# Half of the second key group contracted during the modulation's transfers

## The chip, the core and the metric

The program runs on one core of one Trainium2 chip. The metric is the device time of one execution in microseconds; lower is better. The core's engines are named as the profile names them: PE (matrix multiplications; PEld is its weight load), DVE (vector), ACT (scalar and activation), POOL (general purpose) and SP, whose only work here is to issue transfers. Each runs its own list of instructions in order, and they wait for each other through semaphores. All sums of products go through PSUM, which this kernel hands out in eight banks of 128x512 floats: four named `mm`, two named `sm` and two named `gd` in the stage that is changed.

## The reference

A two-layer backbone over 256 latent tokens and 256 context tokens of width 2048. What matters here is its very beginning: the modulation vectors of layer 0 are computed from `c` and `c_ctx` (a 2048 x 4096 part of `ada_w`), the normalised tokens are scaled and shifted by them, and the result is multiplied by the first columns of `ev_w_in`, the keys `ka` of the gated-delta heads.

```python
sh1, sc1, ... = split(silu(c) @ ada_w[0] + ada_b[0], 6)
h  = rmsnorm(x, norm_mix[0]) * (1 + sc1) + sh1        # 256 latent tokens
hc = the same with ctx and c_ctx                      # 256 context tokens
ka, va, kb, vb, a, b, qa, qb, za = split(h @ ev_w_in) # ka: 1024 columns
k  = l2norm(silu(depthwise_conv(ka)))                 # then the gated delta rule
y  = concat(delta_heads(k, v, q, gates), neighbourhood_attention(qb, kb, vb)) @ ev_w_out
```

Layer 0 goes on with a feed-forward network, layer 1 is a short convolution and another feed-forward network. Everything is float32; a product is made of three matmuls on a high and a low part of both factors (`hi*hi`, `hi*lo`, `lo*hi`).

## The kernel before

**The start.** The 4096 columns of `ada_w` that make shift and scale are taken in eight blocks of 256 + 256 columns. `start_block(b)` (L457) brings one block from memory in four pieces of 128x4x2x256, each by two transfers of 512 KB that SP issues (L463), into a ring of four buffers `araw0`, and multiplies each piece with `cT2` into one `gd` bank (L466). `start_tokens(b)` (L470) turns the bank into what the tokens need: DVE copies it to `mrow` (L472), four small matmuls put the numbers onto partitions (L477), three DVE instructions make shift and scale (L479 to L483), and for the two feature tiles k = 2b, 2b+1 PE transposes the four token tiles (L487), ACT applies shift and scale (L490), and DVE writes the high and low part of `h` (L491, L492). In the profile `araw0` is shown as `araw`, and the high and low parts of h are `hlhi`, `hllo` (latent) and `hchi`, `hclo` (context), `h` for k = 0.

**The contraction.** `fm_stream` (L288) multiplies h with 512 columns of weights for one feature tile k per step: four `mm` banks, and for each bank three weight blocks times two token halves, so 24 matmuls of 128x128 by 256 columns in a step (at k = 0 four of them cover both halves at once). Sixteen steps make one stream; the last two steps are emitted together (TAIL). Its weights come in transfers of 128x1024 floats, 512 KB, issued by SP (L225) into a ring of four `raw` buffers, and are split by ACT (L168, `whi`) and DVE (L234, `wlo`) into rings of three buffers.

In the loop over the blocks (L642) each turn runs `start_tokens(b)`, then two steps of the first stream `s0` (keys, columns 0 to 511) for the tiles just made, then `start_block(b+1)`. After the loop the last two steps of `s0` run (L656), and then the second stream (columns 512 to 1023, L662) runs alone. Each finished stream hands its four banks to `head_evac` (L550), which copies them to `hst`, and puts ten pieces of work (convolution, SiLU, transposes, norms) into a list; `drive` (L393) takes one piece from the list behind each step of whatever stream runs next.

**After it.** The gates of the delta rule (L693), `flush()` of the list (L742), the streams for `va`, `qa` and the others, the chunk matrices and inverses of the delta rule, its scans (L889: matmuls L907, L916, L927, L935, L949 in order), the neighbourhood attention head by head (L1062, L1087), the normalised output of the delta heads (L994, transposes from `o_t`), and the output projection, whose first quarter needs attention heads 0 to 3 and whose second quarter needs the delta heads.

**What sets the order.** The code is written in the order above, but the order on each engine is not that of the code: a scheduler that runs when the program is built simulates a timeline and lets an instruction go ahead of earlier ones when its inputs and buffers are ready there. The order is then fixed.

Of the kernel before, what the change touches and what calls it, by code (L numbers as in the profile page):

```python
# [23 lines left out]
F32 = mybir.dt.float32  # L24
# [80 lines left out]
def body(tc, x, c, ctx, c_ctx, ada_w, ada_b, norm_mix, norm_ffn, ffn_w_gate, ffn_w_up, ffn_w_down,  # L105
# [42 lines left out]
    def mmt():  # L148
        return mm.tile([128, 512], F32, name="mm", tag="mm")
# [135 lines left out]
                        evac(ti, n, ps[ti][n])  # L285
            yield

    def fm_stream(segs, ks, ws, evac):  # L288

        ps = [None] * 4  # L290
        for i, group in grouped(((k, (k, hi, lo)) for k, hi, lo in w_steps(segs, ks)), len(ks)):
            for f in range(4):
                if i == 0:
                    ps[f] = mmt()
                for g, (k, hi, lo) in enumerate(group):
                    a, b = hi[:, f * 128:(f + 1) * 128], lo[:, f * 128:(f + 1) * 128]
                    if i == 0:
                        PE.matmul(ps[f][:, 0:len(ws) * 256], a, h0[:, 0:len(ws) * 256], start=True, stop=False)
                    for j, (wt, mv) in enumerate(((a, h_hi), (a, h_lo), (b, h_hi))):
                        for n, w in enumerate(ws):  # L300
                            if j or i:
                                PE.matmul(ps[f][:, n * 256:(n + 1) * 256], wt, mv(w, k), start=False,  # L302
                                          stop=i == len(ks) - 1 and g == len(group) - 1 and j == 2 and w == ws[-1])
                if i == len(ks) - 1:
                    evac(f, ps[f])
            yield
# [83 lines left out]
            f, args = later.pop(0)  # L390
            f(*args)

    def drive(stream, pump=None, n=1):  # L393
        for _ in stream:
            if later:
                f, args = later.pop(0)
                f(*args)
            if pump:
                pump(n)
# [56 lines left out]

    def start_block(b):  # L457

        pr = gdt()
        for g in range(0, KT, 4):  # L460
            raw = sp.tile([128, 4, 2, 256], F32, name="araw0", tag="araw0", bufs=4)
            for s in range(2):
# [4 lines left out]
                          start=g == 0, stop=g == KT - 4)  # L467
        return pr

    def start_tokens(b, pr):  # L470
        mrow = sp.tile([128, 512], F32, name="mrow", tag="mrow", bufs=2)
        DVE.tensor_copy(mrow, pr)  # L472
        p = smt()
        for s in range(2):
            for f in range(2):
# [5 lines left out]
        DVE.scalar_tensor_tensor(sc0[:, kk, :], p[:, 4:8].rearrange("p (k w) -> p k w", w=2), 1.0,  # L481
                                 bT[:, 16 + 2 * b:18 + 2 * b, None].to_broadcast([128, 2, 2]), op0=OP.add, op1=OP.add)
        DVE.tensor_tensor(sc0[:, kk, :], sc0[:, kk, :], g_mix[0][:, kk, None].to_broadcast([128, 2, 2]), op=OP.mult)  # L483
        for k in range(2 * b, 2 * b + 2):
            p = smt()
            for t in range(4):
                transpose(p[:, t * 128:(t + 1) * 128], xn[:, t, k * 128:(k + 1) * 128])  # L487
            for w in range(2):
                m = sp.tile([128, 256], F32, name="modt", tag="modt", bufs=4)
                ACT.activation(m, p[:, w * 256:(w + 1) * 256], AF.Identity, bias=sh0[:, k, w:w + 1], scale=sc0[:, k, w:w + 1])  # L490
                DVE.tensor_copy(h_hi(w, k), m)  # L491
                DVE.tensor_tensor(h_lo(w, k), m, h_hi(w, k), op=OP.subtract)  # L492

    def token_stats():

# [54 lines left out]
    def head_evac(n, q, c0, done, sums):  # L550
# [1 line left out]
        st_ = {}  # L552

        def f(i_, p):
            st_[i_] = kvp.tile([128, 512], F32, name="hst", tag="hst", bufs=4)[:, 0:n * 128]
            copy(st_[i_], p[:, 0:n * 128])
            if i_ < 3:
                return
# [79 lines left out]

    sums = start_block(0)
    token_stats()  # L640
    s0 = fm_stream([(wv, C_KA, 512)], ks, [0, 1], ka_evac(0))
    for b in range(8):  # L642
        start_tokens(b, sums)
        if b < 7:
            next(s0), next(s0)
            sums = start_block(b + 1)
    st.close()
    rstk = Stack()
# [5 lines left out]
    ACT.dma_start(alog, ev_a_log.rearrange("o d h -> o (d h)").to_broadcast([128, 16]))  # L654
    ACT.dma_start(dtb, ev_dt_bias.rearrange("o d h -> o (d h)").to_broadcast([128, 16]))
    drive(s0)  # L656


    pump = Pump([ada_job(adap, 0, 2, "row", width=512, bufs=AB), ada_job(adap, 0, 3, "sh", width=512, bufs=AB),
                 ada_job(adap, 0, 4, "sc", gamma=g_ffn[0], width=512, bufs=AB)], 1, 1)  # L660

    drive(fm_stream([(wv, C_KA + 512, 512)], ks, [0, 1], ka_evac(1)))  # L662


    abstk = Stack()
# [719 lines left out]
```

## Time and profile before

| what | value |
|---|---|
| median of three runs | 2850.53 us (2845.95 to 2851.98) |
| the profiled execution: its time / its span | 2844.8 us / 2842.7 us |
| outside the span | 2.1 us |
| mean granted clock of PE | 0.988 |
| DVE busy, share of the span | 1902.5 us, 67% |
| ACT busy, share of the span | 1292.9 us, 45% |
| transfers, mean over the span | 239 GB/s |

A row of a group has the line, the engine, the operation, what is written and read, shapes and count; then the busy time in total and the mean of one instruction in ns. A row of a window has its bounds and length, then for PE, PEld, DVE, ACT and POOL the busy time and the number of instructions, then the clock granted to PE, the mean busy share of the transfer engines and GB/s. A row of the chain of waits has the start, the length and what the chain ran through.

### The profile page before, as it was taken

What the parts mean: (1) busy time and instruction counts of PE and PEld (TensorE: products, weight loads), DVE (VectorE), ACT (ScalarE), POOL (GpSimd) and SP (SyncE); (2) the same over time, 40 slices, a digit from 0 to 9 for tenths busy, and PEclk for the clock granted to TensorE, in tenths of its full rate; (3) what the DMA queues carried; (4) which work ended last, traced back from release to release, by engine and by line L of the source; (5) the groups of instructions that cost most, each with busy time, mean ns of one, the idle gap of its engine ahead of it and who ended that gap; (6) DMA issues with size and microseconds to landing.
All of it is one profiled execution on the core that took longest, in us unless ns stands there. A gap on an engine that the chain in (4) does not pass through costs nothing.

```text
span 2842.7 us, 40317 instructions
## 1 busy us (share of the span) xinstructions
PE 2726.7 (96%) x15113; PEld 2281.4 (80%) x15113; DVE 1902.5 (67%) x2599; ACT 1292.9 (45%) x1893; POOL 51.0 (2%) x77
## 2 busy tenths in 40 slices
PE   6899999989989999999999999999999999999997
PEld 3699989888767787888888878888878888888886
DVE  3387767857667887766677768786677544445565
ACT  3267543222354444444445554444444444444554
POOL 0000001000000000000000000000000000000000
PEclk9999999999999999999999999999999999999999
DMA  9955478777758799977788658997569666656663
GB/s 346 311 177 165 141 218 257 236 225 237 210 170 269 253 334 333 326 262 261 264 305 282 199 181 287 318 320 267 185 236 320 216 187 180 192 186 216 191 192 125
DMA packets 284926, 680.77 MB, mean 239 GB/s; under 512 B 57273, under 2 KB 97313, under 8 KB 283323
## 3 DMA queue, kind: packets, MB, share of 16 engines
q1 hardware_dynamic: 262148, 652.48, 69.6%
q10 hardware_dynamic: 22583, 25.73, 2.9%
q8 instruction: 118, 1.93, 0.3%
q14 instruction: 77, 0.63, 0.1%
HBM read 657.63 MB, written 20.48 MB: 239 GB/s over the span
## 4 chain that ended last, share of the span: by engine, by line
PE 66%; DMA 18%; DVE 10%; issue 3%; ACT 2%; SPq 1%; POOL 0%; ACTq 0%; DVEq 0%; POOLq 0%
PE mm L276 16%; PE mm L273 16%; PE mm L274 16%; DMA araw<-in_ada_w_dram 12%; PE mm L302 8%; DVE acc L321 3%; DVE wlo L234 3%; PE sm L187 2%; PE mm L282 2%; PE mm L284 2%; PE mm L283 2%; DMA br<-in_ev_rpb_dram 1%; DMA acc<-in_ada_b_dram 1%; DMA raw<-in_od_w_in_dram 1%; PE gd L466 1%
## 5 line engine op out<-in xcount | busy, mean ns | idle before, releaser
L234 DVE TENSOR_TENSOR wlo<-raw,whi 128x1024 fp32r<-128x1024 f32 x800 | 972.3, 1222 | 476.0 <-ACT whi L168 463.7
L168 ACT ACTIVATE whi<-raw 128x1024 fp32r<-128x1024 f32 x800 | 841.6, 1058 | 907.6 <-PE mm L276 669.4
L321 DVE SCALAR_TENSOR_TENSOR acc<-araw,cT,acc 128x1024 f32<-128x1024 f32 (+1 forms) x416 | 431.2, 1037 | 229.7 <-DMA araw<-in_ada_w_dram 196.3
L274 PE MATMUL mm<-wlo,fhi 128*128 128x512 f32 x1232 | 475.9, 392 | 0.7 <-DVE wlo L234 0.7
L273 PE MATMUL mm<-whi,fhi 128*128 128x512 f32 x1232 | 474.7, 395 | 0.0
L276 PE MATMUL mm<-whi,flo 128*128 128x512 f32 x1232 | 392.9, 393 | 0.0
L274 PEld LDWEIGHTS mm<-wlo,fhi 128*128 128x128 f32 x1232 | 231.5, 188 | 50.7 <-DVE wlo L234 1.4
L276 PEld LDWEIGHTS mm<-whi,flo 128*128 128x128 f32 x1232 | 231.0, 188 | 50.2
L273 PEld LDWEIGHTS mm<-whi,fhi 128*128 128x128 f32 x1232 | 231.6, 188 | 47.9
L273 PE MATMUL mm<-whi,ahi 128*128 128x512 f32 x672 | 259.8, 392 | 0.0
L274 PE MATMUL mm<-wlo,ahi 128*128 128x512 f32 x672 | 259.5, 391 | 0.0
L276 PE MATMUL mm<-whi,alo 128*128 128x512 f32 x672 | 209.7, 392 | 0.0
L302 PE MATMUL mm<-hllo,whi 128*128 128x256 f32 x640 | 181.2, 287 | 0.0
L302 PE MATMUL mm<-hlhi,wlo 128*128 128x256 f32 x600 | 169.7, 288 | 1.8 <-issue 1.4
L302 PE MATMUL mm<-hlhi,whi 128*128 128x256 f32 x600 | 167.2, 289 | 1.0 <-DVE hlhi L491 1.0
L171 ACT ACTIVATE ahi<-prodT 128x256 fp32r<-128x256 f32 x176 | 73.2, 417 | 194.7 <-PE mm L274 186.4
L274 PEld LDWEIGHTS mm<-wlo,ahi 128*128 128x128 f32 x672 | 126.2, 188 | 27.5
L273 PEld LDWEIGHTS mm<-whi,ahi 128*128 128x128 f32 x672 | 126.2, 188 | 27.2
L276 PEld LDWEIGHTS mm<-whi,alo 128*128 128x128 f32 x672 | 126.1, 188 | 27.3
L273 PE MATMUL mm<-whi,dhi 128*128 128x512 f32 x336 | 126.0, 395 | 2.4 <-DVE u_t L1309 1.6
L274 PE MATMUL mm<-wlo,dhi 128*128 128x512 f32 x336 | 127.8, 393 | 0.0
L302 PEld LDWEIGHTS mm<-hllo,whi 128*128 128x128 f32 x640 | 124.1, 194 | 0.5
(391 smaller groups left out, 4014.5 us busy)
## 6 DMA issues: line engine op xcount, KB each, us to landing
araw<-in_ada_w_dram SPq DMA_DIRECT2D x288, 512.0 KB
raw<-in_ffn_w_down_dram SPq DMA_DIRECT2D x176, 512.0 KB
raw<-in_ffn_w_gate_dram SPq DMA_DIRECT2D x160, 512.0 KB
raw<-in_ffn_w_up_dram SPq DMA_DIRECT2D x160, 512.0 KB
raw<-in_ev_w_in_dram SPq DMA_DIRECT2D x112, 512.0 KB
araw<-in_ada_w_dram SPq DMA_DIRECT2D x192, 256.0 KB
raw<-in_od_w_in_dram SPq DMA_DIRECT2D x96, 512.0 KB
raw<-in_ev_w_out_dram SPq DMA_DIRECT2D x32, 512.0 KB
```

The source lines that it names most:

```text
L168: ACT.activation(dst, src, AF.Copy)
L171: ACT.activation(hi, src, AF.Copy)
L187: return PE.transpose(dst, src, ident[:n, :n])
L234: DVE.tensor_tensor(lo, raw, hi, op=OP.subtract)
L273: PE.matmul(ps[ti][n], a, hi[:, n * 512:(n + 1) * 512], start=first, stop=False)
L274: PE.matmul(ps[ti][n], a, lo[:, n * 512:(n + 1) * 512], start=False, stop=False)
L276: PE.matmul(ps[ti][n], b, hi[:, n * 512:(n + 1) * 512], start=False, stop=last)
L282: PE.matmul(ps[ti][n], lh(t), hi[:, c_], start=False, stop=False)
L283: PE.matmul(ps[ti][n], lh(t), lo[:, c_], start=False, stop=False)
L284: PE.matmul(ps[ti][n], ll(t), hi[:, c_], start=False, stop=hi is group[-1][0])
L302: PE.matmul(ps[f][:, n * 256:(n + 1) * 256], wt, mv(w, k), start=False, stop=i == len(ks) - 1 and g == len(group) - 1 and j == 2 and w == ...
L321: DVE.scalar_tensor_tensor(acc, raw, cT[:, k:k + 1], acc, op0=OP.mult, op1=OP.add)
```

## The change

A second stream, `s1`, contracts columns 512 to 767 (half of the second key group) in the loop as well. It needs two banks, and takes them from `gd`; the sums of `start_block` move from `gd` to `sm`. `start_tokens` gets a generator, `both`, that alternates one step of `s0` and one of `s1`, and draws from it at four places: behind the copy to `mrow`, behind the scale, and behind each of the two feature tiles. In block b these are the steps for k = 2b-2 and 2b-1, a block later than before; in block 0 there is nothing to draw. After the loop the last two steps of `s0` and of `s1` run, and then the other half of the second group (columns 768 to 1023) as a stream of 256 columns, behind which `drive` takes a piece of the list only every second step. A step of a 256-column stream has 12 matmuls; its weight transfers have the same 128x1024 floats, now four feature tiles of 256 columns. The buffers `hst` become six.

```diff
-    def fm_stream(segs, ks, ws, evac):
+    def fm_stream(segs, ks, ws, evac, bank=None):
-        ps = [None] * 4
+        nf = sum(s[2] for s in segs) // 128
+        ps = [None] * nf
...
-            for f in range(4):
+            for f in range(nf):
                 if i == 0:
-                    ps[f] = mmt()
+                    ps[f] = (bank or mmt)()
...
-    def drive(stream, pump=None, n=1):
-        for _ in stream:
-            if later:
+    def drive(stream, pump=None, n=1, every=1):
+        for i, _ in enumerate(stream):
+            if later and i % every == every - 1:
...
     def start_block(b):
-        pr = gdt()
+        pr = smt()
...
-    def start_tokens(b, pr):
+    def start_tokens(b, pr, beside):
         mrow = sp.tile([128, 512], F32, name="mrow", tag="mrow", bufs=2)
         DVE.tensor_copy(mrow, pr)
+        next(beside, None)
         p = smt()
...
         DVE.tensor_tensor(sc0[:, kk, :], sc0[:, kk, :], g_mix[0][:, kk, None].to_broadcast([128, 2, 2]), op=OP.mult)
+        next(beside, None)
         for k in range(2 * b, 2 * b + 2):
...
                 DVE.tensor_tensor(h_lo(w, k), m, h_hi(w, k), op=OP.subtract)
+            next(beside, None)
...
-            st_[i_] = kvp.tile([128, 512], F32, name="hst", tag="hst", bufs=4)[:, 0:n * 128]
+            st_[i_] = kvp.tile([128, 512], F32, name="hst", tag="hst", bufs=6)[:, 0:n * 128]
...
-    s0 = fm_stream([(wv, C_KA, 512)], ks, [0, 1], ka_evac(0))
+    ka = [ka_evac(q) for q in range(2)]
+    s0 = fm_stream([(wv, C_KA, 512)], ks, [0, 1], ka[0])
+    s1 = fm_stream([(wv, C_KA + 512, 256)], ks, [0, 1], ka[1], gdt)
+
+    def in_turn(*streams):
+        while True:
+            for s_ in streams:
+                next(s_)
+                yield
+
+    both = in_turn(s0, s1)
     for b in range(8):
-        start_tokens(b, sums)
+        start_tokens(b, sums, both if b else iter(()))
         if b < 7:
-            next(s0), next(s0)
             sums = start_block(b + 1)
...
     drive(s0)
+    drive(s1)
...
-    drive(fm_stream([(wv, C_KA + 512, 512)], ks, [0, 1], ka_evac(1)))
+    drive(fm_stream([(wv, C_KA + 768, 256)], ks, [0, 1], lambda f, p: ka[1](f + 2, p)), every=2)
```

Line numbers behind L300 are one to fifteen higher in the changed kernel. Three places show what becomes of it on the engines.

**PE, between the sums of one block and those of the next** (block 2 of the loop). `cT` times `araw` are the sums of a block, `sm<-cs,mrow` the small matmuls of `start_tokens`, `sm<-cs,xn` the transposes of the tokens; `mm` and `gd` rows with `whi` or `wlo` are steps of `s0` and `s1`. Before:

```order
L466 MATMUL gd<-araw_421,cT_120 32x512 x4
L466 MATMUL gd<-araw_428,cT_120 32x512 x4
L466 MATMUL gd<-araw_435,cT_120 32x512 x4
L477 MATMUL sm<-cs,mrow 128x2 x4
L187 MATMUL sm<-cs,xn 128x128 x8
L466 MATMUL gd<-araw_533,cT_120 32x512 x4
L302 MATMUL mm<-hlhi,whi 128x256 x4
```

After, block 7, where the last sums are followed by the rest of the contraction:

```order
L303 MATMUL mm<-hlhi,wlo 128x256
L480 MATMUL sm<-cs,mrow 128x2 x4
L187 MATMUL sm<-cs,xn 128x128 x4
L303 MATMUL mm<-hchi,wlo 128x256
...
L303 MATMUL gd<-hlhi,wlo 128x256
L187 MATMUL sm<-cs,xn 128x128 x4
L303 MATMUL gd<-hchi,wlo 128x256
L303 MATMUL mm<-hlhi,whi 128x256 x4
```

Before, the small matmuls stood directly behind the last sums of their block, and all 48 matmuls of `s0` behind the transposes. Now stream matmuls stand between the last sums and the small matmuls (21 to 26 of them), between the two groups of transposes, and between the sums of the next block; 72 of them belong to a block.

**SP, around the last piece of the modulation's columns.** `araw` with 128x4x256 is a transfer of a block, `raw` a transfer of weights. Before:

```order
L463 DMA araw_1023<-in_ada_w_dram 128x4x256 x2
L463 DMA araw_1030<-in_ada_w_dram 128x4x256 x2
L225 DMA raw<-in_ev_w_in_dram 128x2x512 x2
L320 DMA araw<-in_ada_w_dram 128x512 x3
L317 DMA acc<-in_ada_b_dram 1x512
```

After:

```order
L225 DMA raw<-in_ev_w_in_dram 128x4x256
L464 DMA araw_1117<-in_ada_w_dram 128x4x256 x2
L464 DMA araw_1124<-in_ada_w_dram 128x4x256 x2
L464 DMA araw_1131<-in_ada_w_dram 128x4x256 x2
L464 DMA araw_1138<-in_ada_w_dram 128x4x256 x2
L225 DMA raw<-in_ev_w_in_dram 128x4x256 x2
L225 DMA raw<-in_ev_w_in_dram 128x2x512
L321 DMA araw<-in_ada_w_dram 128x512 x3
```

Counted from the top of SP's list, 12 transfers of weights stood ahead of the last piece of `araw` before, and 14 do now.

**PE, at the end of the delta rule's scans.** `gd<-state,kT`, `gd<-state,qT`, `gd<-R,xdT` and `gd<-vn,AT` are the four matmul groups of the last scan step, `kb,qb` are scores of the attention, `PT,vb` its values, and `mm` rows with `yhi` or `ylo` are the first quarter of the output projection. Before:

```order
L916 MATMUL gd<-state,qT 128x128 x4
L927 MATMUL gd<-R,xdT 128x128 x4
L1101 MATMUL sm<-PT,vb 128x256 x4
L1077 MATMUL sm<-kb,qb 128x512
L1078 MATMUL sm<-bq,cs 128x256
L949 MATMUL gd<-vn,AT 128x128 x4
...
L273 MATMUL mm<-whi,yhi 128x512 x4
L274 MATMUL mm<-wlo,yhi 128x512 x2
L276 MATMUL mm<-whi,ylo 128x512 x2
```

After:

```order
L276 MATMUL mm<-whi,ylo 128x512 x2
L187 MATMUL sm<-cs,s 128x128 x4
L964 MATMUL gd<-vn,AT 128x128 x4
L922 MATMUL gd<-state,kT 128x128 x4
L187 MATMUL sm<-cs,s 128x128 x4
L931 MATMUL gd<-state,qT 128x128 x4
L942 MATMUL gd<-R,xdT 128x128 x4
L1116 MATMUL sm<-PT,vb 128x256 x4
L964 MATMUL gd<-vn,AT 128x128 x4
L1092 MATMUL gd<-kb,qb 128x512
```

Before, the 48 matmuls of the output projection's first quarter (of 512 columns each) stood behind the last `vn,AT` of the scans. Now they stand ahead of the last `vn,AT` but one, and behind the scans only attention is left.

## The prediction

> **What bounds the kernel now.** I read the page's engine shares first, then windows, the chain of waits, and the waits of PE and SP inside the stage that is changed.
>
> ```profile
> PE 2726.7 (96%) x15113; PEld 2281.4 (80%) x15113; DVE 1902.5 (67%) x2599; ACT 1292.9 (45%) x1893; POOL 51.0 (2%) x77
> 60.00:120.00 60.00, 54.07 (x418) 37.24 (x417) 19.37 (x52) 12.17 (x20) 0.00 (x0) 0.97 1.08 351
> 40.00:140.00 100.00, 89.96 (x672) 62.16 (x673) 38.15 (x100) 23.07 (x39) 4.01 (x3) 0.98 1.01 328
> 140.00:193.00 53.00, 53.00 (x443) 52.80 (x442) 41.88 (x68) 33.66 (x80) 0.00 (x0) 1.00 0.63 193
> 480.00:720.00 240.00, 221.34 (x1851) 198.69 (x1850) 161.79 (x292) 63.82 (x121) 9.80 (x12) 0.97 0.77 236
> 720.00:960.00 240.00, 219.85 (x1046) 175.09 (x1046) 166.94 (x309) 116.69 (x225) 2.07 (x3) 0.96 0.67 211
> ```
>
> PE is busy 96% of the span, and the change neither adds nor removes a matmul. So the time can only fall by PE idle time that goes. While the modulation's columns arrive (40 to 140 us) PE is idle 10.0 of 100 us, with the transfer engines full at 351 GB/s. In the stage behind it (140 to 193, the second key group) it is never idle. Most other idle time before 960 us lies in the delta rule and the attention: 18.7 us in one window, 20.1 us in the next.
>
> ```profile
> 54.82 1.02 PE sm L477 x8
> 67.18 1.02 PE sm L477 x8
> 69.22 9.48 DMA araw<-in_ada_w_dram
> 97.13 1.04 PE sm L187 x8
> 132.61 2.76 PE gd L466 x24
> 135.39 0.70 DVE mrow L472
> 136.23 1.02 PE sm L477 x8
> 138.78 6.20 PE mm L302 x48
> 169.66 23.02 PE mm L302 x192
> ```
>
> These are rows of the chain. L477, the small matmuls, marks each block: from block 2 (67.18) to block 7 (136.23) five blocks take 69.05 us, **13.8 us each**. PE's own work in a block is 48 stream matmuls of 23.02/192 = 0.120 us (5.76 us), 32 records of sums at 2.76/24 = 0.115 us (3.68), the small matmuls (1.02) and the transposes (1.04): **11.5 us**. The chain runs through transfers of `araw` there. PE has 2.3 us to spare per block, and the transfers set the pace.
>
> **The change, part by part.**
>
> *Matmuls moved.* Of the 432 stream matmuls that stood behind block 7's small matmuls, 283 remain (counted from the orders; a 512-column matmul counts as two). That takes 149 x 0.120 = 17.9 us from the tail. The price is paid in the blocks: block 1 has 66 ahead of its small matmuls instead of 48 (+2.2 us, from 54.8 to 57.0), and from block 1 to block 7 stand 485 - 66 = 419. If PE never waits, block 7's small matmuls start at 57.0 + 419 x 0.120 + 6 x (3.68 + 1.02 + 1.04) = 57.0 + 50.2 + 34.4 = 141.6, that is 5.4 us later than 136.2. The tail then takes 283 x 0.120 + 1.0 + 1.0 + 2 (small matmuls, transposes, and those of the first heads) = 38.0 us. The second key group ended at 169.66 + 23.02 = 192.7 and would end at 179.6: **At most 13.1 us** earlier.
>
> *Transfers moved.* Two more weight loads stand ahead of the last `araw`.
>
> ```profile
> araw<-in_ada_w_dram SPq DMA_DIRECT2D x64, 512.0 KB
> 124.78 10.34 SPq L225 DMA_DIRECT2D raw<-in_ev_w_in_dram  x2
> SPq L463 <- PE gd L466: 22.0, 8, 3.8
> ```
>
> 2 x 0.524 MB at the 351 GB/s of the window is **3.0 us**. The last sums ended at 135.4; they would end at 138.4, and 26 stream matmuls (3.1 us) now stand between them and the small matmuls: 141.5. The limit by transfers and the limit by PE fall on the same point, so neither has slack. The new loads have the shape 128x4x256 that `araw` has (two of them to a piece), and those run at 351 GB/s, so I add nothing for shorter runs. SP already waits for PE's sums to free an `araw` buffer, 22.0 us in eight waits, at most 3.8; a transfer takes 9.5 us to land (the 69.22 row), so PE can free a buffer some microseconds late before the engines run dry. From nothing to 3.8 us for each of six blocks; I take nothing, as the transfer share is full in spite of those waits.
>
> *What fills the gaps.*
>
> ```profile
> PE sm L477 <- DVE mrow L472: 4.7, 5, 1.0
> PE gd L466 <- DMA araw<-in_ada_w_dram: 3.7, 4, 1.8
> PE sm L187 <- DVE xn L505: 1.0, 2, 0.5
> PE mm L302 <- DVE hlhi L491: 1.0, 2, 0.5
> L490 ACT ACTIVATE modt<-sm,sh,sc 128x256 f32<-128x256 f32 x32 | 15.7, 563 | 35.5 <-PE sm L187 35.5
> ```
>
> PE's waits between 40 and 140 us are for the copy `mrow` (4.7 us), for `araw` (3.7 us) and for h. The copy takes 0.70 us and has 21 to 26 matmuls in front of its reader now, so those 4.7 us go. h is used later, so those waits go too. The waits for `araw` remain where transfers are late. The sums' new place in `sm` adds a wait: the bank is free only when ACT has read it (two instructions of 0.56 us). Behind it on PE stand the sums, hence SP's next transfers. In the order, stream matmuls stand between; bounds 0 and 1.1 us per block, and I take 0, nearest to the stream matmuls that cover it.
>
> *The weight splits.*
>
> ```profile
> L234 DVE TENSOR_TENSOR wlo<-raw,whi 128x1024 fp32r<-128x1024 f32 x800 | 972.3, 1222 | 476.0 <-ACT whi L168 463.7
> L168 ACT ACTIVATE whi<-raw 128x1024 fp32r<-128x1024 f32 x800 | 841.6, 1058 | 907.6 <-PE mm L276 669.4
> ```
>
> ACT and DVE need 1.06 + 1.22 = 2.3 us for a split, and two streams share three buffers. The second stream reuses the buffer that it has just finished, so its split falls between two of its steps; there the order has 24 to 34 other stream matmuls (2.9 us or more). Four such places: 0 if covered, 9.1 us if each stands bare. They also leave DVE less to do later: 41.9 us of 53 in the tail, less about four splits (4.9) is 37.0 of the 38.0 us that the tail now lasts. DVE becomes nearly full there, with pieces of `head_evac` ahead of splits.
>
> For all of this I let 4 us of the 13.1 remain as waits (a number chosen between 0 and 9.1): **-9.0 us** at the end of the second key group, nine tenths of the 10.0 us of idle time that the window records.
>
> *What comes after.* The gates of the delta rule and all behind them stand later in PE's order. The first matmul of the gates has 911 stream matmuls before it now, and will have 1061; the first inverse 1976, then 2175. By 0.120 us that is 18.0 and 23.9 us later, less the 9.0 won: the delta rule starts 9 to 15 us later than before (its gates at 220 + 9 = 229).
>
> ```profile
> 220.04 1.26 PE sm L732 x12
> 744.39 1.05 PE L927 MATMUL gd<-R,xdT 128*128 128x128 f32 x8
> 803.93 1.06 PE L907 MATMUL gd<-state,kT 128*128 128x128 f32 x8
> 807.84 1.16 PE L927 MATMUL gd<-R,xdT 128*128 128x128 f32 x8 [0.59 <-DVE R L910]
> 813.84 1.13 PE L949 MATMUL gd<-vn,AT 128*128 128x128 f32 x8 [1.82 <-DVE o_t L921]
> 842.42 1.11 PE gd L187 x4
> ```
>
> The scans must end before the output projection can go on (842.4, transposes of the normalised output, 28.6 us behind the last scan matmul). Before, the first quarter of that projection (96 half-width matmuls, 11.5 us) filled this gap. In the new order it stands ahead of the last scan step, which fills the scans instead and leaves the gap emptier. Price: 0 if the scan steps simply run closer, 11.5 us if nothing replaces it. The last step took 813.84 - 803.93 = 9.9 us, while steps from 744.4 to 807.8 took 63.5/4 = 15.9 us: they were spread by other work, so they can run closer. I take the lower part: **+3.0 us**.
>
> *Sum.* -9.0 + 3.0 = -6.0 us: 2844.8 - 6.0 = 2838.8 for the profiled execution. That execution was 5.7 us under the median of 2850.5, and the change is compared with runs like the median: **2844.5 us**. The rest of the kernel behind 960 us has the same order but for single rows; nothing there.
>
> **A rule beside a row.**
>
> ```profile
> 110.00:120.00 10.00, 10.00 (x64) 6.79 (x57) 2.70 (x8) 1.61 (x4) 0.00 (x0) 0.86 1.09 353
> ```
>
> PE's granted clock was 0.86 here and 0.97 from 60 to 120. The Trainium skill, "TensorE: Matmul & The Clock Gate", section "What's actually happening", says that an idle window of about 3.4 us drops the clock to half. No wait of PE in this stage lasted over 1.8 us, so the trace has drops where the rule has none. If the denser order removes all of them, 0.03 x 60 = 1.8 us more is won; this enters the first rival alone.
>
> **The rivals.**
>
> *All of it stays.* The delta rule catches up at no cost and the waits are few: -13.1 - 1.8 = -14.9 at the extreme, typically -11: 2839.5. For it: 38.8 us of idle time between 480 and 960 that a moved chain could use. Against it: two limits at the same point.
>
> *Given back.* The start wins 9 us, and the scans, later in the order, return 7 to 9 of the 11.5: -1, 2849.5. For it: 28.6 us between scans and projection with one filler fewer. This includes that the change doesn't do what it says, because PE waits for `araw` where it waited before.
>
> *Slower.* One mechanism, the delta rule's chain. It starts up to 15 us later than before; if its steps can't run closer than their 15.9 us, the whole lateness reaches 842 us in place of the win: +6 to +15, I put +7: 2857.5. It decides once the lateness at the scans' start is more than the steps can make up, 4 x (15.9 - 9.9) = 24 us at best. Against it: that margin.
>
> **How the numbers follow.** Forecast -6 has 0.40, "all stays" 0.15, "given back" 0.30, "slower" 0.15. About 0.2%, 5.7 us, is what a measurement of this kernel can tell from no change. Forecast cases lie between -3 and -9; three quarters of them under -5.7 count as faster: 0.30 + 0.15 = 0.45. Same: 0.10 + 0.30 + 0.02 of the slower case = 0.42. Slower: 0.13. The range takes in -15.5 and leaves the worst of the last rival out, +5.5: 2835 to 2856.
>
> **What would show it.** Block marks (small matmuls) about 14.2 us apart and block 7's near 142; the last transposes and 192 stream matmuls of the second key group over by 184; PE idle between 40 and 140 at 3 us or less; the first gates' matmuls near 229; the transposes of the normalised output by 836. Wrong, if block marks are 15 us or more apart, if SP's waits for PE's sums exceed 22 us by much, if PE waits for `wlo` between 140 and 185, or if the normalised output comes at 842 or later.

## The result, and the profile after

| | before | after |
|---|---|---|
| median of six runs | 2846.98 us (2842.55 to 2851.98) | 2863.76 us (2856.03 to 2871.37) |
| ratio of the times, 95% interval | | 1.0053 (1.0038 to 1.0069) |
| profiled execution: time / span | 2844.8 / 2842.7 us | 2856.03 / 2854.2 us |
| mean granted clock of PE | 0.988 | 0.985 |

The changed kernel is **slower by 0.53%**; the forecast was 2844.5 us, with 2856 as the upper end. The profiled execution is the fastest of the six, and its span is 11.5 us longer than the one before. In the experiments below, one execution (of e10) took 9226.19 us; it is in no ratio.

First the page's engine line and windows of the changed kernel: bounds and length, busy time and instructions of PE, PEld, DVE, ACT and POOL, then PE's clock, the transfer engines' share and GB/s.

```profile
PE 2730.8 (96%) x15113; PEld 2282.0 (80%) x15113; DVE 1898.4 (67%) x2599; ACT 1298.7 (45%) x1897; POOL 52.7 (2%) x77
60.00:120.00 60.00, 58.51 (x460) 43.12 (x456) 19.20 (x50) 12.49 (x20) 0.00 (x0) 0.97 1.01 324
40.00:140.00 100.00, 97.25 (x749) 70.06 (x753) 37.52 (x92) 22.73 (x37) 0.00 (x0) 0.98 1.03 331
140.00:193.00 53.00, 53.00 (x447) 51.04 (x440) 40.74 (x64) 29.12 (x68) 4.02 (x3) 1.00 0.49 146
140.00:340.00 200.00, 193.41 (x1594) 189.20 (x1587) 156.58 (x332) 142.49 (x315) 13.98 (x21) 0.99 0.52 160
340.00:440.00 100.00, 87.14 (x1052) 84.32 (x1050) 65.50 (x106) 38.72 (x57) 2.97 (x4) 0.91 0.71 211
440.00:960.00 520.00, 478.04 (x3258) 410.50 (x3257) 358.92 (x666) 195.47 (x375) 21.07 (x31) 0.96 0.72 225
```

The same view of the kernel before, for the windows that the prediction doesn't show:

```profile
140.00:340.00 200.00, 195.97 (x1620) 194.03 (x1619) 156.53 (x328) 134.51 (x304) 8.81 (x18) 0.99 0.52 158
340.00:440.00 100.00, 95.50 (x1201) 92.30 (x1200) 73.67 (x124) 46.99 (x71) 4.96 (x8) 0.98 0.73 225
440.00:960.00 520.00, 479.20 (x3199) 411.39 (x3199) 361.26 (x666) 196.66 (x378) 19.54 (x28) 0.96 0.72 225
```

The start does what was hoped: PE idle between 40 and 140 us falls from 10.0 to 2.75 us. From 140 to 340 us idle time grows by 2.6, and **from 340 to 440 us from 4.5 to 12.9 us, with the clock at 0.91 in place of 0.98**. In that one window PE does about 87.14 x 0.91 = 79 us of full-speed work, where it did 95.50 x 0.98 = 94: some 14 us are lost there. From 440 to 960 us the idle time is equal within 1.2 us. Over the span idle time grows from 116.0 to 123.4 us, and the same matmuls are 4.1 us longer busy: together the 11.5 us.

Next PE's marks in time: the small matmuls (L480) of blocks 1, 2 and 7, the first matmul behind the second key group (L692), the first of the gates (L747), the last scan step (L964) and the transposes of the normalised output.

```profile
55.50 0.95 PE L480 MATMUL sm<-cs,mrow 128*128 128x2 f32 x8
71.92 0.95 PE L480 MATMUL sm<-cs,mrow 128*128 128x2 f32 x8
...
146.78 0.95 PE L480 MATMUL sm<-cs,mrow 128*128 128x2 f32 x8
184.81 0.28 PE L692 MATMUL sm<-h,abw 128*64 128x256 f32 x1
227.88 0.53 PE L747 MATMUL sm<-g_t,cs 128*128 128x32 f32 x4
839.04 1.05 PE L964 MATMUL gd<-vn,AT 128*128 128x128 f32 x8
861.81 1.07 PE L187 MATMUL gd<-cs,o_t 128*128 128x128 f32 x8
```

And of the kernel before, the first matmul behind the second key group and the first transposes of the normalised output:

```profile
192.52 0.28 PE L677 MATMUL sm<-h,abw 128*64 128x256 f32 x1
852.53 0.66 PE L187 MATMUL gd<-cs,o_t 128*128 128x128 f32 x4
```

The second key group ends at 184.8 instead of 192.5, **7.7 us earlier**. The gates come at 227.9 (219.9 before). The first inverse of the delta rule, in the view of its line, comes 31.3 us later:

```profile
L869 PE MATMUL gd<-xd,n x384: 190/218/268, 375.7 to 612.3; 32*32 32x32 f32 x128, 64*64 64x64 f32 x64
```

was that line before, and after the change it is

```profile
L884 PE MATMUL gd<-xd,n x384: 184/218/267, 407.0 to 638.1; 32*32 32x32 f32 x128, 64*64 64x64 f32 x64
```

The last scan step is 25.2 us later (839.0 against 813.84), the normalised output 9.3 us. What lies ahead of the first inverse is a triangular solve on DVE: 62 steps that follow one another (`sub_tmp`, `zsol`, 31 of each) and a copy (`lsol`). DVE's groups from the first of them to the last, before (311.1 to 367.8 us):

```profile
L545 DVE SCALAR_TENSOR_TENSOR cv<-hst,evcT,cv 128x508 f32<-128x508 f32 (+1 forms) x20 | 14.1, 742 | 0.0
L234 DVE TENSOR_TENSOR wlo<-raw,whi 128x1024 fp32r<-128x1024 f32 x10 | 12.2, 1220 | 3.6 <-ACT whi L168 3.6
L828 DVE TENSOR_TENSOR zsol<-zsol,sub_tmp 128x31 f32<-128x31 f32 (+15 forms) x31 | 10.6, 341 | 0.7
L826 DVE TENSOR_TENSOR sub_tmp<-lsol,zsol 128x31 f32<-128x31 f32 (+15 forms) x31 | 10.5, 340 | 2.4 <-DMA n<-nd 1.7
```

and after (319.3 to 384.7 us):

```profile
L550 DVE SCALAR_TENSOR_TENSOR cv<-hst,evcT,cv 128x508 f32<-128x508 f32 (+1 forms) x32 | 22.6, 741 | 0.0
L234 DVE TENSOR_TENSOR wlo<-raw,whi 128x1024 fp32r<-128x1024 f32 x14 | 17.1, 1219 | 3.9 <-ACT whi L168 3.9
L843 DVE TENSOR_TENSOR zsol<-zsol,sub_tmp 128x31 f32<-128x31 f32 (+15 forms) x31 | 10.6, 341 | 0.7
L841 DVE TENSOR_TENSOR sub_tmp<-lsol,zsol 128x31 f32<-128x31 f32 (+15 forms) x31 | 10.6, 340 | 2.0 <-DMA n<-nd 1.3
```

The solve itself is the same 22 us. Between its steps stand the convolutions (`cv`) of the value heads and the weight splits (`wlo`): 20 and 10 before, **32 and 14 after**. The likely reason is that PE had run ahead with the streams and the value heads' work was ready earlier; the fixed order of DVE has it in the middle of the solve: 12 x 0.741 + 4 x 1.22 = 13.8 us more of it, less some rope products that stood there before. The solve takes 65.4 us instead of 56.6. It starts 8.2 us later too; ACT writes the keys of the two groups later (e2 below has the same late keys, and the same late start):

```profile
214.85 0.63 ACTq L621 DMA_DIRECT2D kd<-hq  x1
```

The first group's write stood at 186.55 us before, and the second group's moved from 259.5 to 269.3. Behind the solve, POOL clears `xd`, which has the solve's buffer, only when that buffer's last writes to memory have landed: at 371.77 before, at 397.46 after, 12 us after they were issued and not 4. From the solve's end to that clearing the transfer engines are 0.86 busy at 268 GB/s, where they were 0.49 busy at 153: weight loads and a write of the value heads (`vd`, 1024 KB, issued at 383.82) run beside those writes. So of the 31.3 us at the first inverse 8.2 come from the solve's later start, 8.7 from its length, and 14.4, nearly half, from behind it.

PE's waits between 340 and 440 us name who is missed:

```profile
PE mm L299 <- ACT nst L1054: 8.6, 2, 5.5
PE gd L884 <- DMA xd<-dz: 3.0, 1, 3.0
```

A row has the total in us, the number and the longest. `nst` are two buffers for copying the qb, kb and vb streams out of PSUM. Before, PE waited there for neither; its longest total was 2.5 us. PE comes to the qb stream, and the buffers aren't free. So PE meets two things too early: the copies, and the delta rule.

### The profile page after: what moved, and what is told of

Its sections match the earlier page's. It is cut to its first block, busy times and chain, and to the rows that moved or that the text cites. A ratio compares the mean times of both kernels' runs of the same rounds, so it can differ in the third digit from the quotient of the medians.

```text
span 2854.2 us, 40344 instructions
## 1 busy us (share of the span) xinstructions
PE 2730.8 (96%) x15113; PEld 2282.0 (80%) x15113; DVE 1898.4 (67%) x2599; ACT 1298.7 (45%) x1897; POOL 52.7 (2%) x77
## 4 chain that ended last, share of the span: by engine, by line
PE 58%; DMA 7%; DVE 4%; issue 1%; ACT 1%; POOL 0%; ACTq 0%; DVEq 0%; SPq 0%
PE mm L274 17%; PE mm L273 17%; PE mm L276 17%; DMA araw<-in_ada_w_dram 4%; PE mm L282 2%; DVE wlo L234 2%; PE mm L284 2%; PE mm L283 2%; PE sm L187 2%; DVE acc L322 1%; DMA raw<-in_od_w_in_dram 1%; DMA acc<-in_ada_b_dram 0%; PE sm L336 0%; DMA raw<-in_ffn_w_gate_dram 0%; DMA raw<-in_ffn_w_down_dram 0%
## 5 line engine op out<-in xcount | busy, mean ns | idle before, releaser
L303 PE MATMUL mm<-hllo,whi 128*128 128x256 f32 x608 | 174.5, 291 | 0.0
L303 PE MATMUL mm<-hlhi,wlo 128*128 128x256 f32 x570 | 160.2, 290 | 0.0
```

## The experiments

Five theories were tried. START: the loss is made in the start. ORDER: any other order of the same work moves the time by some 10 us. CHAIN: later keys make all behind them later. STAGE: the `nst` buffers. SOLVE: the crowd on DVE inside the solve. Each kernel was timed beside the kernel before on one chip. The rounds ran on different chips, so across rounds the ratios are to be compared. Milestones are of the profiled executions, in us; cv and wlo are counted inside the solve.

| kernel | block 7 | keys written | gates | solve, from to | cv, wlo | first inverse | last scan matmul | ratio to before (95%) |
|---|---|---|---|---|---|---|---|---|
| before | 136.2 | 187, 260 | 219.9 | 311.1 367.7 | 20, 10 | 375.7 | 814.7 | 1 |
| the change | 146.8 | 215, 269 | 227.9 | 319.3 384.6 | 32, 14 | 407.0 | 839.8 | 1.0053 (1.0038 to 1.0069) |
| e2 | 136.2 | 211, 268 | 227.8 | 319.8 369.9 | 19, 8 | 378.6 | 820.8 | 1.0008 (0.9993 to 1.0022) |
| e3 | 138.8 | 191, 263 | 223.5 | 314.8 370.4 | 20, 10 | 378.7 | 813.7 | 1.0015 (1.0004 to 1.0026) |
| e4 | 137.2 | 188, 261 | 220.9 | 312.8 368.4 | 20, 10 | 377.0 | 816.2 | 1.0007 (0.9991 to 1.0023) |
| e5 | 155.3 | 222, 278 | 235.9 | 332.5 399.0 | 32, 15 | 419.6 | 867.7 | 1.0098 (1.0076 to 1.012) |
| e6 | 145.4 | 213, 268 | 226.3 | 319.2 383.6 | 32, 14 | 404.4 | 829.9 | 1.0012 (1.0 to 1.0023) |
| e7 | 137.9 | 188, 261 | 221.5 | 315.1 370.7 | 20, 10 | 377.9 | 810.1 | 0.996 (0.9932 to 0.9988) |
| e8 | 146.1 | 214, 268 | 227.0 | 318.9 365.9 | 17, 8 | 375.9 | 831.3 | 1.0014 (1.0001 to 1.0027) |
| e9 | 146.2 | 214, 269 | 227.3 | 319.2 366.4 | 17, 8 | 377.5 | 817.3 | 0.9997 (0.9985 to 1.0009) |
| e10 | 136.7 | 186, 260 | 220.4 | 311.9 366.9 | 17, 10 | 375.1 | 809.0 | 0.998 (0.9966 to 0.9995) |
| e11 | 135.6 | 185, 259 | 219.3 | 310.6 364.5 | 17, 10 | 376.0 | 811.0 | 1.0012 (1.0001 to 1.0024) |
| e12 | 146.1 | 242, 254 | 199.3 | 326.0 375.9 | 13, 12 | 389.2 | 817.2 | 0.9995 (0.9983 to 1.0006) |
| e13 | 136.2 | 205, 265 | 183.4 | 319.5 390.2 | 32, 15 | 410.1 | 842.1 | 1.0068 (1.0042 to 1.0093) |
| e14 | 146.1 | 214, 270 | 227.1 | 320.4 353.6 | 1, 6 | 363.3 | 792.7 | 0.9967 (0.9954 to 0.998) |
| e15 | 136.6 | 187, 260 | 220.3 | 312.2 352.1 | 1, 8 | 362.3 | 800.8 | 0.999 (0.9974 to 1.0006) |

One thing stands in the table that the theories don't name. In the four kernels with 32 convolutions inside the solve (the change, e5, e6, e13) the first inverse comes 20 to 22 us after the solve's end, in all others 7 to 13. The transfer engines between the solve's end and the clearing of `xd` are 0.76 to 0.86 busy in those four, 0.45 to 0.57 in the others. So the crowd goes along with a slow way of the results through memory; no run separates the two, and the name SOLVE covers both here.

**e2, the heads at half pace in the kernel before.**

```diff
-    drive(fm_stream([(wv, C_KA + 512, 512)], ks, [0, 1], ka_evac(1)))
+    drive(fm_stream([(wv, C_KA + 512, 512)], ks, [0, 1], ka_evac(1)), every=2)
```

> The kernel before, and one thing of the change alone: behind the steps of the second key group's stream a piece of head work is taken only every second step. No matmul is moved in the start; the write of the first key group's heads to memory stands 18 rows later on ACT. Theory CHAIN (the heads' work on ACT and DVE feeds the delta rule; the change lets that chain start later, and the PE time won at the start is lost again where PE has nothing left but the chain): the second key group ends at 192 to 194 us as before, the first keys are written 10 us or more after the 186.6 us of before, the last scan matmuls come 8 us or more after 814.7, and the time is 4 to 12 us above the kernel before. Theory START (the loss is made in the start itself, by transfers that wait): no difference, within 3 us. Theory ORDER (any other order of the same work after the start moves the time by some 10 us either way, without a common cause): either sign, not following the keys.

Keys and gates come as late as in the change (211 and 268, 227.8 us), and the time doesn't move. **CHAIN in this form falls**: late keys alone cost next to nothing. Here the solve isn't crowded (19 and 8), and it ends at 370.

**e3, a block later without the second stream; e4, other banks alone.** In e3 `s0` is drawn behind the two feature tiles only. Against the change (e3), and against the kernel before (e4):

```diff
-    both = in_turn(s0, s1)
+    both = in_turn(s0)
...
-    drive(fm_stream([(wv, C_KA + 768, 256)], ks, [0, 1], lambda f, p: ka[1](f + 2, p)), every=2)
+    drive(fm_stream([(wv, C_KA + 512, 512)], ks, [0, 1], ka[1]))
```

```diff
-        pr = gdt()
+        pr = smt()
...
-name="hst", tag="hst", bufs=4)
+name="hst", tag="hst", bufs=6)
```

> The change without the second stream: the first key group is contracted a block later (its two steps drawn behind the feature tiles of the next block), the sums are in the other PSUM banks, the second key group runs behind the loop as 512 columns, as before. Theory CHAIN: the first group's heads begin when the first stream ends, some 3 to 6 us later than the 143.1 us of before, the fill of the start is smaller than in the change (PE idle between 40 and 140 us 4 to 9 us), and the time is within 5 us of the kernel before. Theory START: PE idle between 40 and 140 us falls little, and the time is 5 to 10 us above before, as in the change. Theory ORDER: either sign.

> The kernel before with only the sums of the start in the other PSUM banks and six buffers for the copied heads. Nothing of the work or its place in the program's text is moved; what the scheduler makes of it differs in single rows and in stretches behind. Theory CHAIN: keys and gates within 4 us of before, and the time within 4 us of before (0.2%). Theory START: the same, unless the sums wait for the banks: then SP's waits for the sums rise above 25 us and the time by 3 us. Theory ORDER: 5 us or more from before, either way, though the keys come in time.

PE idle between 40 and 140 us is 11.0 us in e3 (4 to 9 were expected) and 11.3 in e4, so without the second stream the gaps stay. Both times are within 0.2% of before. Neither banks nor delay nor another order as such makes the loss: START and ORDER lose most of their ground.

**e5, the first stream in time.**

```diff
-    both = in_turn(s0, s1)
+    both = in_turn(s1)
...
+            next(s0), next(s0)
             sums = start_block(b + 1)
```

> The change, but the first stream runs its two steps of a block right behind that block's tokens, as before; only the second, narrow stream runs a block later. Theory CHAIN: the first group's heads begin 4 to 8 us earlier than the 155.9 us of the change, its keys are written before 208 us instead of at 214.9, the last scan matmuls come 5 us or more before the 839.8 of the change, and the time falls by 3 to 10 us from the 2864 of the change. Theory START: the start is as long as in the change or longer, and the time is within 3 us of the change. Theory ORDER: either sign.

A miss for all: the start became longer (block 7 at 155.3 us), so the first heads came later, not earlier. It still fits SOLVE (32 and 15, 66.5 us, and the slowest time), though the longer start has its part in that time.

**e6 and e7, four `nst` buffers**, in the change and in the kernel before.

```diff
-NST = 2
+NST = 4
```

> The change, with four instead of two buffers for the copies of the qb, kb and vb streams (nst). Theory STAGE (PE runs through the head streams ahead of the heads' work, comes to the qb stream earlier and stands there for a free nst buffer; that is the 8.6 us wait at 385 to 403 us, with the clock at half behind it): the wait falls under 3 us, and the time falls by 5 to 12 us from the 2864 of the change. Theory SOLVE (DVE puts 32 convolution steps and 14 weight splits of the head streams between the steps of the triangular solve, 20 and 10 before; inverses, scans and attention come later from there): the solve still ends at 380 to 388 us, the last scan matmuls still after 832, and the time is within 4 us of the change.

> The kernel before with four nst buffers, the control of the run above. Both theories: PE's waits for nst in the kernel before are 2.0, 5.3 and 0.4 us, all behind 440 us; at most those go, so 0 to 8 us under the kernel before. If it gains as much as the change does from the same edit, the buffers have nothing to do with the change's loss.

The change falls from 1.0053 to 1.0012, some 12 us by the ratios, the upper end of what STAGE expected; SOLVE had expected at most 4. Its solve stays crowded, and PE still waits 4.9 us for `nst`, where STAGE expected under 3 of the 8.6. But the kernel before gains 0.4% by the same edit, as much as the change. By the mark set in e7's expectation the buffers then aren't what sets the two kernels apart: they are a limit of both, and equal buffers leave the change 0.5% behind. The waits for `nst` are a way in which a part of the loss is paid.

**e8 and e9, the convolutions of the second value group queued on DVE behind the solve** (a rule on DVE's issue order, nothing waits for a result), with two and with four `nst` buffers.

```diff
-        DVE.tensor_copy(lsol, zsol.rearrange("p r c -> p c r"))
+        solved.append(DVE.tensor_copy(lsol, zsol.rearrange("p r c -> p c r")))
...
             def front(i):
+                if c0 == 8 and q == 1:
+                    with tc.issue_after(solved[0].ins):
+                        cvs[i] = conv_silu(st_[i], n // 2, c0 + q * 4 + i)
+                    return
```

> The change, with one rule on DVE's order: the convolutions of the second value group are queued behind the last step of the first triangular solve. The order then has 16 convolution steps and 8 splits inside the solve instead of 32 and 14. Theory SOLVE: the solve takes 45 to 52 us instead of 65.4 and ends at 365 to 372 us instead of 384.6, the first inverse comes 12 us or more before 407, the last scan matmuls before 832 instead of 839.8, and the time falls by 6 to 14 us, to the kernel before or under it. Theory STAGE: the value heads end later, PE waits longer for nst (over 12 us between 370 and 430), and the time stays at the change's or rises.

> The change with both edits, the convolutions behind the solve and four nst buffers. Theory SOLVE: within 3 us of the run with the convolutions behind the solve alone. Theory STAGE: within 3 us of the run with four buffers alone. If each carries a part of the loss, this run is below both, and 4 to 8 us below the kernel before, as the 6.1 us won at the start would then be kept.

DVE's groups inside the solve of e8 (318.9 to 366 us):

```profile
L550 DVE SCALAR_TENSOR_TENSOR cv<-hst,evcT,cv 128x508 f32<-128x508 f32 (+1 forms) x17 | 12.1, 744 | 0.0
...
L234 DVE TENSOR_TENSOR wlo<-raw,whi 128x1024 fp32r<-128x1024 f32 x8 | 9.8, 1221 | 1.8 <-ACT whi L168 1.8
```

The solve takes 47.0 us, the first inverse is back at 375.9, and the ratio falls from 1.0053 to 1.0014: **SOLVE holds**, and the longer waits for `nst` that STAGE expected don't come. The two edits aren't additive. Each alone took some 11 us from the change; both together (e9, 0.9997) come to 5 us under either alone and to the time of the kernel before, not to 4 to 8 us below it.

**e10 and e11, the same edits in the kernel before.**

> The kernel before with both edits: convolutions of the second value group behind the solve, four nst buffers. Its order has 16 convolution steps inside the solve instead of 19. It is the control of the change with both edits (2844.3 us). Theory SOLVE + STAGE as the whole loss: it stands 3 to 8 us above the change with both edits, that is at 2847 to 2852, since the change then keeps its 6 us at the start. If it stands at 2833 to 2840 instead, like the kernel before with four buffers alone (2836.9), the change loses 5 us or more by something that neither edit mends.

> The kernel before with the convolutions of the second value group behind the solve, two nst buffers. Three fewer convolution steps (2.2 us) inside the solve. Theory SOLVE (the 14 us that this rule gains in the change come from the crowd of DVE work which the change brought there): at most 4 us from the kernel before, either way. If it gains 8 us or more here too, the rule helps for another reason and says nothing of the change.

The rule gains nothing in the kernel before (1.0012), where it moves only 3 convolution steps out of the solve; in the change it moves 15. So what it gains in the change is what the change brought. But e10 (0.998) stands below e9 (0.9997), though the intervals overlap: with both edits the change still doesn't keep its win, and SOLVE and STAGE together, as far as these edits mend them, aren't the whole loss.

**e13, the same crowd without the change; e12, the gates early.** In both the gates are written ahead of the second group's last stream: e13 in the kernel before with four `nst` buffers, e12 in e9. The lines from `abstk = Stack()` to `abstk.close()` move as they are:

```diff
+    abstk = Stack()
...
+    gates()
+    abstk.close()
     drive(fm_stream([(wv, C_KA + 512, 512)], ks, [0, 1], ka_evac(1)))
-    abstk = Stack()
...
-    gates()
-    abstk.close()
```

> The kernel before with four nst buffers and the gates written ahead of the second key group's stream. The start is untouched (block marks as before). The order happens to have 32 convolution steps and 15 splits inside the solve, as in the change, where the kernel before with four buffers has 20 and 10. It tells SOLVE from all theories that look in the start. Theory SOLVE: the solve takes 62 us or more instead of 55.6 and the first inverse comes 10 us or more after the 378 of the kernel before with four buffers, though the gates come 20 us earlier; the time rises by 5 to 14 us above that kernel's 2837. Theory START or keys alone: the time is at 2837 or below.

> The change with both edits, and the gates of the delta rule written ahead of the narrow stream instead of behind it. In the order the gates stand at 844 half-width stream matmuls instead of 1061, but ACT's write of the first keys stands 36 rows later. If the gates are what holds the delta rule back: first inverse before 370 us and 3 to 8 us under 2844. Theory SOLVE: what counts is when the keys of both groups are there and what stands inside the solve (12 convolution steps, 12 splits, about as with both edits): the solve ends at 362 to 374 us and the time is within 5 us of 2844.

e13's DVE groups inside the solve (319.5 to 390.3 us):

```profile
L545 DVE SCALAR_TENSOR_TENSOR cv<-hst,evcT,cv 128x508 f32<-128x508 f32 (+1 forms) x32 | 22.4, 743 | 0.0
L234 DVE TENSOR_TENSOR wlo<-raw,whi 128x1024 fp32r<-128x1024 f32 x15 | 18.3, 1219 | 3.1 <-ACT whi L168 3.1
```

The start is untouched and the gates come 38 us earlier than in e7, yet the solve takes 70.7 us, the first inverse comes 32 us later, and the time is 27 us above e7 (2863.66 against 2836.92), about twice the upper end of what was expected. It is the sharpest of the runs for SOLVE, with one reservation: moving the gates also moves the keys (205 and 265 us, where e7 has 188 and 261), and 27 us is more than the crowd costs the change. e12 makes the same move in the changed kernel without the crowd, and the time stays where it was (0.9995, e9 0.9997): early gates alone neither win nor cost. Its solve ended at 375.9, just behind the 362 to 374 expected, and its first inverse came 12 us later than in e9, at no loss of time. Why that costs nothing there wasn't traced.

**e14 and e15, both value groups behind the solve**, in e9 and in e10.

```diff
-                if c0 == 8 and q == 1:
+                if c0 == 8:
...
-name="hst", tag="hst", bufs=6)
+name="hst", tag="hst", bufs=7)
```

(In e10 the second edit starts from four buffers.) Open was why e9 keeps nothing. PE's waits from 340 to 440 us in e9, and its window:

```profile
PE gd L890 <- DMA xd<-dz: 11.7, 5, 3.9
340.00:440.00 100.00, 88.16 (x1117) 85.43 (x1116) 68.74 (x118) 40.41 (x59) 3.52 (x6) 0.91 0.69 209
```

and in e10:

```profile
PE gd L875 <- DMA xd<-dz: 0.5, 1, 0.5
340.00:440.00 100.00, 94.06 (x1201) 90.78 (x1201) 71.02 (x120) 45.32 (x67) 4.53 (x6) 1.00 0.73 222
```

The solve ends at the same time in both (366.4 and 366.9). PE is ahead in e9 (busy 304.1 us of the first 340, 298.6 in e10, at a clock of 0.99 in both) and waits 11.7 us for the results, with the clock at 0.91 against 1.00. The profiled execution of e9 is the slowest of its ten (2853.52 us, median 2844.34), so these two rows show more of a difference than the medians have. If that is all, a solve that ends earlier gives the win back.

> The change with four nst buffers and the convolutions of both value groups queued on DVE behind the solve (seven hst buffers so that the banks can be emptied meanwhile). No convolution and 6 splits stand inside the solve. If the date of the solve's end decides: the solve takes 32 to 38 us, ends at 351 to 358 us instead of 366, PE's waits for xd between 340 and 440 us fall from 11.7 to under 4 us, and the time is 2833 to 2840, that is 2 us or more below the kernel before with the same edits. If something else of the change eats the win: PE waits elsewhere before 440 us for the missing 8 us, and the time stays 3 us or more above the kernel before with the same edits.

> The control: the kernel before with four nst buffers, seven hst buffers and the same rule. No convolution and 8 splits inside the solve, which ends at 351 to 358 us too. If the date decides, PE was not waiting for it here (1.9 us at that place with both edits), so the earlier end gains little: 2835 to 2842, within 4 us of the 2839.5 of the kernel before with both edits.

The window and the waits of e14:

```profile
PE gd L890 <- DMA xd<-dz: 2.2, 2, 2.0
340.00:440.00 100.00, 96.90 (x1216) 93.84 (x1215) 79.64 (x135) 52.36 (x86) 10.73 (x11) 0.98 0.71 218
```

The solve takes 33.2 us and ends at 353.6, the waits for `xd` fall to 2.2 us, and the change keeps its win: 2836.67 against 2845.45 us of e15, where the same rule moves the solve's end as far (352.1 us) and gains nothing over e10. e15 is even above the 2835 to 2842 expected. The profiled spans differ by 6.8 us (2836.6 and 2843.4), about what was won at the start. The two ratios' intervals overlap by a little (0.9954 to 0.998 and 0.9974 to 1.0006). e14 is below the kernel before and the change. It is not below e7, the kernel before with four buffers alone (0.996, from five executions), so against the best form of the kernel before no win is shown.

## Why the prediction was wrong, point by point

**What bounds the start: half right.** The idle time fell to 2.75 us (3 or less was forecast), the waits for `mrow` are gone, and PE never waits from 140 to 193 us, for `wlo` or anything else (53.00 of 53 us busy). But the blocks are 15.0 us apart, (146.78 - 71.92)/5, and not 14.2, and block 7's small matmuls came at 146.8, not 142. What failed is the price of PE's own work. The count of 419 stream matmuls from block 1 to block 7 was right; the prediction priced all of PE's work there at 84.6 us, and it took 91.3. PE was idle for only 1.9 us of these (89.43 of 91.28 us busy), so 4.8 of the 6.7 us are busy time above the price, of which the clock of 0.98 explains some 1.7. The kernel before had shown it: between the same marks PE was busy for 73.08 us, where the same prices give 6 x 11.5 = 69.0. SP's waits after the change, to 190 us:

```profile
SPq L225 <- DVE hlhi L495: 26.7, 5, 13.2
SPq L464 <- PE sm L467: 19.3, 14, 3.9
SPq L225 <- DVE wlo L234: 16.5, 8, 3.6
```

SP stands longer for weight loads (L225) whose buffers aren't free, 24.6 us between 40 and 140 where it was 16.8, and the `araw` loads (L464) are queued behind them: 324 GB/s from 60 to 120 us, where 351 ran before. As PE was busy nearly throughout, that cost little: the pace is PE's now, and taking nothing for SP did no harm.

**End of the second key group, -9.0 us: near, and partly by luck.** -7.7 us were measured. The 4 us that the prediction let remain were meant as waits, on a scale set by the weight splits. No split was waited for; the rest of the contraction took 38.0 us (146.78 to 184.81), as forecast without any wait. In their place the blocks took 5.2 us more than forecast (146.8 against 141.6).

**The gates at 229: right** (227.9).

**The delta rule 9 to 15 us later: the step that failed.** It was worked out from the number of stream matmuls that stand ahead of the delta rule on PE, times 0.120 us. That gave the gates. It left out DVE, between gates and first inverse. The order put 12 more convolutions and 4 more splits into the solve (+8.7 us), which already began 8.2 us later, and the results were in place later again: 31.3 us at the first inverse. In the sum this lateness had no term but the scans' +3.0; some 14 us were lost at 340 to 440 us, ahead of the scans, where the sum has nothing. e2 shows that the late keys and gates alone are absorbed, e8 that the crowd is what makes the solve late, e13 that the same crowd costs time without the change. Why the results take so long behind a crowded solve stays open.

**Filler that is drawn ahead is missing later: not asked.** The prediction counted 149 half-width matmuls (17.9 us) moved out of the tail as a gain on PE, and looked for missing filler only at the output projection. By e9, e10, e14 and e15 it was PE's lead itself that met the solve too early at 340 to 440 us: the change keeps its win in e14, where the solve ends 13 us earlier than in e9, and not in e9. This rests on overlapping intervals, and e12 keeps e9's time with a later solve, so the lead is the best reading and not a proof.

**+3.0 us for the scans: near in size, not by its working.** From 440 to 960 us PE's idle time grew by 1.2 us. But of the margin of 24 us, by which steps were to run closer, only 6 were used: 31.3 us of lateness at the first inverse are still 25.2 at the last scan step, and only behind the scans is more made up, as the output is 9.3 us late. And the row at 842.42 us was misread. Those transposes are of the attention's `s`; the normalised output came at 852.53. It now comes at 861.81, where 836 was forecast and 842 named as the mark of failure.

**The sum.** -7.7 us at the start, then some 19 us back to +11.2 us for the profiled execution; the medians are 16.8 us apart. The rival "slower" named the delta rule's lateness and a price of +6 to +15, but had it reach the output through the scans, where next to nothing was lost; the loss came ahead of them, while PE waited for the solve and the copies. It got 0.15, because its margin was taken from scan steps and not from the solve. Behind 960 us next to nothing changed, as forecast (30.9 us idle to the end of the span before, 32.3 after).

## What to carry to other kernels

A gap that is filled with work from later is a loan: look up what that work covered, and date the chain that it covered on every engine in it, not on the one that waits. Where a scheduler fixes the order, count what stands between the steps of a serial piece on its own engine before and after, as 12 more fillers of 0.74 us and 4 of 1.22 us stood in the solve here, 13.8 us against a win of 7.7. When two kernels differ by such a thing, give both the same relief before comparing them: four buffers made the change look mended, and made the kernel before faster still.

## What the runs showed of the hardware

A wait of PE can cost more than itself, as these traces have the clock at half for a while around many of the waits. Two matmuls of the changed kernel, with the wait ahead of each in brackets, in the order of time:

```profile
392.75 0.58 PE L299 MATMUL mm<-h,whi 128*128 128x256 f32 x1 [5.49 <-ACT nst L1054]
402.12 0.39 PE L299 MATMUL mm<-h,whi 128*128 128x256 f32 x1 [3.07 <-ACT nst L1054]
```

and two windows there:

```profile
389.00:405.00 16.00, 9.19 (x54) 8.98 (x55) 2.79 (x4) 1.43 (x4) 0.96 (x1) 0.74 0.71 194
403.50:406.90 3.40, 3.40 (x18) 3.36 (x16) 0.00 (x0) 0.84 (x2) 0.00 (x0) 0.51 0.65 135
```

In the second PE is busy throughout, at a clock of 0.51: 1.7 us lost after the wait had ended. The trace's clock record has such stretches of 3.41 us or two or three times that, between 40 and 960 us ten before and eleven after, and each of them begins in or behind a wait of 1.0 to 6.3 us; other waits of such length, one of 1.84 us at 93.2 before the change, have none. The Trainium skill, "TensorE: Matmul & The Clock Gate", section "What's actually happening", has the clock drop after an idle window of about 3.4 us; the length of the stretches agrees with that window, and a wait of 1.01 us at 108.0 us before the drop at 109.5 (before the change) doesn't.
